# A hybrid GLA, FoX and memory layer on one core: GpSimd in source order in the gates, FoX decay rows loaded and masked in two steps, DRAM sums paced otherwise

## The chip, the cores and the metric

The kernel runs on one core of one Trainium2 chip. The metric is the device time of one execution in microseconds (us). Before the change three runs took 825.73, 826.78 and 827.77 us; their median is 826.78 us. The traces are of single executions, and times within a trace count from its start.

The core's engines run beside each other, each through its own list of instructions, and wait for one another by semaphores. TensorE (PE in the profile) multiplies matrices into PSUM, the memory of its results. VectorE (DVE) and ScalarE (ACT) work element by element on PSUM and SBUF, the main on-chip memory. GpSimd (POOL) does a little of the same and issues DMA transfers, among them those that add what they bring to what stands at the target. SyncE (SP) does nothing but issue transfers.

## The reference, cut to what matters

One layer of an encoder over 512 frames of width 1024: a gated linear attention (GLA), a forgetting attention (FoX) and an attention to 256 memory tokens, merged by three gates, then an output projection and a squared-ReLU MLP. All in float32.

```python
u = rmsnorm(h, g_mix[l])
proj = u @ w_in[l]
(gq, gk, gv, gg, ga, fq, fk, fv, ff, mq, gates) = split_cols(proj, PROJ_SIZES)
...
o_gla = rmsnorm(o_gla, g_gla_head[l]) * jax.nn.silu(gg.reshape(B, S, GLA_HEADS, GLA_DV))
y_gla = o_gla.reshape(B, S, GLA_V) @ w_gla_o[l]
...
# FoX, for each block of 128 queries
s = jnp.einsum('bhqd,bhkd->bhqk', qi, kh).astype(jnp.float32) * scale
s = s + Fi[..., None] - F[:, :, None, :]
mask = k_pos[None, :] <= q_pos[:, None]
p = jax.nn.softmax(jnp.where(mask, s, -jnp.inf), axis=-1)
...
gt = jax.nn.sigmoid(gates.reshape(B, S, N_BRANCH, D))
merged = gt[:, :, 0] * y_gla + gt[:, :, 1] * y_fox + gt[:, :, 2] * y_mem
h = h + merged @ w_out[l]
u2 = rmsnorm(h, g_ffn[l])
h = h + jnp.square(jax.nn.relu(u2 @ w_ff1[l])) @ w_ff2[l]
return rmsnorm(h, g_final)
```

The change touches the FoX scores, the GLA, the three gate projections with their merge, and the beginning of the output projection.

## The kernel before

Precision. Each operand of a matmul is split into a high part (a rounded copy, made by a ScalarE cast: `hi`, `whi`, `f1h`) and a low part (what is left, made by a VectorE subtraction: `lo`, `wlo`, `f1l`). A product is three matmuls, high by high, high by low and low by high (`mm3`, lines 162 to 165). So before TensorE can use a weight tile of 128 by 1024, the tile has to land, be cast (line 153 or 1087) and be subtracted (line 154 or 1091).

Fewer multiplications. The large products are not done block by block but in seven products of sums of blocks, as in Strassen's scheme. So weights are needed in sums: "11", "12", "21" and "22" name the quarters of a weight matrix that such a sum adds up.

Order. TensorE runs in the order of the source. The other engines' lists are put in order by a scheduler, except inside `in_order()` (line 131), which chains each instruction of VectorE, ScalarE and SyncE behind the one before it in the source. All the gates stand inside one such block (line 1237). GpSimd isn't in the chain, and the scheduler orders it.

FoX, about 60 to 150 us of the trace. Eight heads are worked in four pairs j. For head h, `decay_bcast` (line 628) loads a row of decays, broadcast to 128 partitions, into a tile nFb (two buffers) by a DMA that ScalarE issues; the mask is added to it by two VectorE instructions (line 640). `fox_scores(j)` computes the scores of a pair and subtracts nFb, `fox_turn(h)` transposes the probabilities and splits them (PTh, PTl), and `fox_values(h)` multiplies them by V and writes oT (line 703), which is split into ofh and ofl. These steps are listed with a number of filler matmuls each and woven with matmuls of projections. Loads and masks are one step, `fox_rows`.

GLA, about 220 to 295 us, is woven in the same manner from a list of steps with their shares of fillers.

Sums in DRAM. For the MLP some sums of weight blocks are made in DRAM ahead of their use (the tensors T): 40 DMAs of GpSimd, listed by `sum_ops` (line 105), of which 35 come early and five late. `next_sum` (line 115) is called at each weight cast. From the eighth on it lets the next two of the list go, each waiting for that cast. When `late_on` is set, it takes from the five late ones, which also wait for the last merge on GpSimd.

Gates, 296 to 424 us. Three gates g (0 FoX, 1 memory, 2 GLA) take seven rounds n each, in the order 1, 2, 5, 3, 6, 7, 4. A round is two tiles of 128 frames, 24 matmuls. The round (2, 4) is put among the rounds of the GLA output ("Y", 1), ("Y", 0) and of the output projection ("O", 1), ("O", 0). A round reads two weight tiles c. Those of rounds 1, 5, 6, 7 and 4 are built in place in four SBUF tiles wb: `pair[m][c]`, where m is 0 or 1. By their numbers in the listings, wb_473 and wb_474 are pair[0], wb_475 and wb_476 are pair[1]. Gate g builds rounds 1, 5, 6 and 4 in pair[g % 2] and round 7 in the other pair. SyncE loads the first block, and GpSimd adds the others, each by an accumulate DMA (`plus`, line 1073). `low(r, c)`, called a round ahead of the matmuls, makes the low part; behind rounds 1, 5 and 6 it issues the accumulate for the next round on the same tile: "12" behind round 1 (for round 5), "22" behind 5 (for 6), "21" behind 6 (for 4). Behind the matmuls of round 5 the other pair gets its "22", for round 7. The results pass through tiles ct (`evac`) and a tanh. For gates 1 and 2, VectorE multiplies by the branch (line 1167) and GpSimd adds the product to acc (`merge`, line 1168).

Of the kernel before, what the change touches and what calls it, by code (L numbers as in the profile page):

```python
# [58 lines left out]
def hybrid_block(ctx, tc, chunks, wst, memT, xT, xN, gffn, gfin, wup, cst, out):  # L59
    nc = tc.nc  # L60
# [55 lines left out]
    def next_sum(after):  # L116

        chunk_n[0] += 1
        if chunk_n[0] <= 7:
            return  # L120
        for to, src, add_ in islice(sums[len(late_on)], 2):
            with tc.issue_after(merged[0]) if late_on else ExitStack():
                if add_:
                    d = nc.gpsimd.dma_start(to, src, accum_op=ALU.add, max_dma_last_dim=8192)
                else:
                    d = nc.gpsimd.dma_start(to, src)
            tc.add_manual_dep(d.ins, after.name, mybir.DependencyInfo(mybir.DependencyClass.Sync, mybir.DependencyReason.DATA),
                              reason="pace")

    @contextmanager  # L130
    def in_order():

        traced = nc.cur_bb.bb.instructions
        last, behind = traced[-1], {}
        yield
        for i in traced[next(k for k in reversed(range(len(traced))) if traced[k] is last) + 1:]:
            if i.engine in (mybir.EngineType.DVE, mybir.EngineType.Activation, mybir.EngineType.SP):
                if i.engine in behind:
                    tc.add_manual_dep(i, behind[i.engine].name, mybir.DependencyInfo(
                        mybir.DependencyClass.NoSync, mybir.DependencyReason.DATA), reason="order")  # L140
                behind[i.engine] = i
# [360 lines left out]
    with pool("fox") as xp:  # L502
# [122 lines left out]
        live, rows = {}, {}  # L625
# [7 lines left out]
        def fox_rows(j):  # L633
            for e in range(2):
                if j:
                    rows[2 * j + e] = decay_bcast(2 * j + e, nc.scalar)
                nFb = rows[2 * j + e]
                for b in (slice(1, 2), slice(5, 8)):
# [95 lines left out]
        mem_rows()  # L734
        fox_rows(0)
        fox_scores(0)
# [3 lines left out]

        gvg = v_chunks(OFF["gv"], lambda t, ps: nc.scalar.copy(gv[:, t, :], ps))
        T, V_, R, A = fox_turn, fox_values, fox_rows, fox_scores
        steps = [(R, 1, 0), (T, 0, 5), (V_, 0, 0), (T, 1, 5)]
        for j in range(1, 4):
            more = 1 + (j == 3)
            steps += [(A, j, 4 * more), (V_, 2 * j - 1, 5 * more)] + [(R, j + 1, 0)] * (j < 3)
            steps += [(T, 2 * j, 5 * more), (V_, 2 * j, 0), (T, 2 * j + 1, 5 * more)]
        steps.append((V_, 7, 0))
# [129 lines left out]
    with pool("gla") as lp:  # L878
# [115 lines left out]
        def u_lefts():  # L994
# [5 lines left out]
        steps = (  # L1000
            (decays, (0,), 13), (key_turn, (0,), 5), (gla_scores, (0,), 2), (decays, (1,), 9), (key_turn, (1,), 4),
            (gla_values, (0,), 0), (gla_scores, (1,), 8), (gla_turn, (0,), 0), (gla_turn, (1,), 4), (gla_values, (1,), 10),
            (u_lefts, (), 0), (gate_ready, (0,), 0), (gla_turn, (2,), 6), (gate_ready, (1,), 0), (gla_turn, (3,), 0))
# [27 lines left out]
    with pool("outp") as op_:  # L1031
# [204 lines left out]
        hN, now = [], [rounds[0]]  # L1236
        with in_order():
            for n in range(2):
# [4 lines left out]
            for i, r in enumerate(rounds):  # L1243
# [5 lines left out]
                if r == ("Y", 0):  # L1249
                    late_on.append(1)  # L1250
                    hN += [h_tile(t, "h") for t in range(NT)]
# [12 lines left out]
                for t in range(n):  # L1264
# [7 lines left out]
                    if t == 0:  # L1272
                        for x in parts:
                            merge(*x)
                        for x in due:
                            high(*x)
                            low(*x)
                        go(after, i)
                evac(r, n - 1)
        u2j = up.tile([P, 2, 4, 4, 256], F32R, tag="uhl", name="u2")  # L1280
# [747 lines left out]
```

## Time and profile before

| | us |
|---|---|
| median of three runs | 826.78 |
| the profiled execution | 827.7 |
| its span on the core | 825.9 |
| TensorE busy within the span | 800.9 |
| VectorE busy | 607.5 |
| ScalarE busy | 459.6 |
| GpSimd busy | 102.9 |

The profiled execution is 0.9 us above the median. Its span is shorter than its time by 1.8 us, which lie before the first instruction and behind the last. The mean clock granted to TensorE was 0.993 of full speed.

How such rows read. A row of the timeline or of the waits has the start (us), the busy time (us), engine, line, operation, the tile written, an arrow and the tiles read, the shapes, xN for the number of instructions in it, and in brackets the engine's idle time just before it and what ended that. A line such as L1087 is a line of the kernel before; where a helper stands there, several callers share it. An engine with a q (SPq, POOLq) is the queue of a DMA that the engine issued.

### The profile page before, as it was taken

What the parts mean: (1) busy time and instruction counts of PE and PEld (TensorE: products, weight loads), DVE (VectorE), ACT (ScalarE), POOL (GpSimd) and SP (SyncE); (2) the same over time, 40 slices, a digit from 0 to 9 for tenths busy, and PEclk for the clock granted to TensorE, in tenths of its full rate; (3) what the DMA queues carried; (4) which work ended last, traced back from release to release, by engine and by line L of the source; (5) the groups of instructions that cost most, each with busy time, mean ns of one, the idle gap of its engine ahead of it and who ended that gap; (6) DMA issues with size and microseconds to landing.
All of it is one profiled execution on the core that took longest, in us unless ns stands there. A gap on an engine that the chain in (4) does not pass through costs nothing.

```text
span 825.9 us, 11694 instructions
## 1 busy us (share of the span) xinstructions
PE 800.9 (97%) x4375; PEld 681.3 (82%) x4375; DVE 607.5 (74%) x945; ACT 459.6 (56%) x733; POOL 102.9 (12%) x135
## 2 busy tenths in 40 slices
PE   9999999999999998988999999999999999999996
PEld 7788877888888776756888879987998899889985
DVE  6868787375545886567666467879799779888896
ACT  7756655435543445444543347865577466647764
POOL 0001111211100120134301000011001100110011
PEclk9999999999999999999999999999999999999998
DMA  9354879999922229866937932798857865896643
GB/s 357 131 176 178 327 264 240 248 337 246 339 90 77 104 76 203 224 136 196 213 98 257 271 110 102 254 239 204 245 188 170 216 243 167 190 237 229 172 81 124
DMA packets 40489, 164.39 MB, mean 199 GB/s; under 512 B 4848, under 2 KB 5552, under 8 KB 38064
## 3 DMA queue, kind: packets, MB, share of 16 engines
q0 software_dynamic: 10784, 61.87, 34.4%
q1 hardware_dynamic: 28288, 97.81, 32.9%
q10 hardware_dynamic: 1360, 3.96, 1.3%
q8 instruction: 34, 0.56, 0.3%
q14 instruction: 23, 0.19, 0.1%
HBM read 161.50 MB, written 35.68 MB: 239 GB/s over the span
## 4 chain that ended last, share of the span: by engine, by line
PE 45%; DMA 8%; DVE 5%; issue 4%; ACT 2%; POOL 0%; POOLq 0%; SPq 0%; DVEq 0%; ACTq 0%
PE mm L1321 11%; PE mm L164 7%; PE mm L165 7%; PE mm L163 7%; DMA wb<-in_wst_dram 4%; PE a L164 3%; PE a L165 3%; PE a L163 3%; PE mm L1650 3%; DMA b<-in_wst_dram 2%; DMA raw<-in_wst_dram 2%; PE mm L1651 1%; DVE lo L1091 1%; DVE lo L1438 1%; DVE f0l L1091 0%
## 5 line engine op out<-in xcount | busy, mean ns | idle before, releaser
L154 DVE TENSOR_TENSOR wlo<-raw,whi 128x1024 fp32r<-128x1024 f32 x38 | 46.5, 1224 | 39.6 <-ACT whi L153 39.6
L1381 DVE TENSOR_TENSOR lo<-raw,hi 128x1024 fp32r<-128x1024 f32 x52 | 63.5, 1223 | 15.6 <-ACT hi L1380 15.5
L1380 ACT CAST hi<-raw 128x1024 fp32r<-128x1024 f32 x52 | 54.4, 1048 | 35.6 <-PE mm L1321 14.2
L1321 PE MATMUL mm<-u,hi 128*128 128x256 f32 x384 | 65.1, 283 | 0.0
L153 ACT CAST whi<-raw 128x1024 fp32r<-128x1024 f32 x38 | 39.9, 1050 | 43.7 <-PE mm L164 14.7
L1700 POOL DMA_DIRECT2D b<-in_wst_dram x30 | 25.6, 855 | 265.3 <-DVE lo L1381 131.1
L163 PE MATMUL mm<-uhl,whi 128*128 128x512 f32 x144 | 57.6, 400 | 0.0
L1321 PEld LDWEIGHTS mm<-u,hi 128*128 128x128 f32 x384 | 56.8, 191 | 0.3
L165 PE MATMUL mm<-uhl,wlo 128*128 128x512 f32 x144 | 56.3, 391 | 0.0
L164 PE MATMUL mm<-uhl,whi 128*128 128x512 f32 x144 | 56.1, 390 | 0.0
L164 PE MATMUL mm<-lo,ch 128*128 128x512 f32 (+1 forms) x132 | 51.2, 388 | 0.4 <-DVE lo L1381 0.4
L163 PE MATMUL mm<-hi,ch 128*128 128x512 f32 (+1 forms) x132 | 51.0, 386 | 0.0
L165 PE MATMUL mm<-hi,cl 128*128 128x512 f32 (+1 forms) x132 | 50.9, 386 | 0.0
L1321 PE MATMUL mm<-u2s,hi 128*128 128x256 f32 x288 | 47.6, 283 | 0.0
L1321 PE MATMUL mm<-u,lo 128*128 128x256 f32 x192 | 47.5, 283 | 0.0
L1091 DVE TENSOR_TENSOR lo<-wb,hi 128x1024 fp32r<-128x1024 f32 x22 | 30.2, 1384 | 20.8 <-ACT hi L1087 20.7
L1380 ACT CAST hi<-b 128x1024 fp32r<-128x1024 f32 x26 | 27.3, 1048 | 29.3 <-PE mm L165 19.2
L1321 PEld LDWEIGHTS mm<-u2s,hi 128*128 128x128 f32 x288 | 41.8, 192 | 0.3
L1381 DVE TENSOR_TENSOR lo<-b,hi 128x1024 fp32r<-128x1024 f32 x26 | 31.7, 1223 | 10.7 <-ACT hi L1380 10.7
L164 PE MATMUL a<-lo,ch 128*128 128x512 f32 (+1 forms) x96 | 37.2, 388 | 0.8 <-DVE lo L1438 0.8
L163 PE MATMUL a<-hi,ch 128*128 128x512 f32 (+1 forms) x96 | 37.0, 386 | 0.0
L165 PE MATMUL a<-hi,cl 128*128 128x512 f32 (+1 forms) x96 | 37.0, 385 | 0.0
(508 smaller groups left out, 2317.5 us busy)
## 6 DMA issues: line engine op xcount, KB each, us to landing
raw<-in_wst_dram SPq DMA_DIRECT2D x108, 512.0 KB
raw<-T SPq DMA_DIRECT2D x32, 512.0 KB
b<-in_wst_dram POOLq DMA_DIRECT2D x32, 512.0 KB, 5.8
T<-in_wst_dram POOLq DMA_DIRECT2D x12, 1024.0 KB, 17.4
wb<-in_wst_dram POOLq DMA_DIRECT2D x22, 512.0 KB, 6.7
b<-in_wst_dram SPq DMA_DIRECT2D x16, 512.0 KB
T<-in_wst_dram POOLq DMA_DIRECT2D x12, 512.0 KB, 8.8
wb<-in_wst_dram SPq DMA_DIRECT2D x12, 512.0 KB
```

Of the source, the lines that this page charges most:

```text
L153: cast = nc.scalar.copy(hi, raw)
L154: low_now[0] = nc.vector.tensor_tensor(lo, raw, f(hi), op=ALU.subtract).ins
L163: nc.tensor.matmul(ps, lh, rh, start=start, stop=False, skip_group_check=on)
L164: nc.tensor.matmul(ps, lh, rl, start=False, stop=False, skip_group_check=on)
L165: nc.tensor.matmul(ps, ll, rh, start=False, stop=stop, skip_group_check=on)
L1091: nc.vector.tensor_tensor(lo, source(r, c), f(hi), op=ALU.subtract)
L1321: nc.tensor.matmul(ps[:, a, :], x[:, a, k, :], y[:, s, k, :], start=start, stop=stop, skip_group_check=go is not None)
L1380: split_now[0] = nc.scalar.copy(hi, raw).ins
L1381: split_now[1] = nc.vector.tensor_tensor(lo, raw, f(hi), op=ALU.subtract).ins
L1438: return nc.vector.tensor_tensor(lo, raws[n, i], f(hi), op=ALU.subtract).ins
L1650: nc.tensor.matmul(ps, wh[:, a, k, :], u[:, :, k, :], start=k == 0, stop=False, skip_group_check=True)
L1700: nc.gpsimd.dma_start(to[i], wst[index["B", q, i, x]], accum_op=ALU.add)
```

## The change

It has four parts.

- `in_order` takes further engines, and the block of the gates names GpSimd: its accumulates and merges stand in the order of the source there.
- FoX: `fox_rows` only issues the loads of a pair's two decay rows, right behind the scores of the pair before; a new step `fox_masks` adds the masks, behind `fox_values(2j)`.
- GLA: three units of filler, nine matmuls, move from `gla_scores(1)` to `gla_values(0)`.
- DRAM sums: one sum a cast up to the 14th cast and two from the 15th, where it was two from the eighth; the five late ones go one a cast, and from the end of round (2, 7) instead of the start of ("Y", 0).

```diff
--- before.py
+++ after.py
@@ -118,7 +118,7 @@
         chunk_n[0] += 1
         if chunk_n[0] <= 7:
             return
-        for to, src, add_ in islice(sums[len(late_on)], 2):
+        for to, src, add_ in islice(sums[len(late_on)], 1 if late_on or chunk_n[0] <= 14 else 2):
             with tc.issue_after(merged[0]) if late_on else ExitStack():
                 if add_:
                     d = nc.gpsimd.dma_start(to, src, accum_op=ALU.add, max_dma_last_dim=8192)
@@ -128,13 +128,14 @@
                               reason="pace")
 
     @contextmanager
-    def in_order():
-
+    def in_order(*others):
+
+        engines = (mybir.EngineType.DVE, mybir.EngineType.Activation, mybir.EngineType.SP, *others)
         traced = nc.cur_bb.bb.instructions
         last, behind = traced[-1], {}
         yield
         for i in traced[next(k for k in reversed(range(len(traced))) if traced[k] is last) + 1:]:
-            if i.engine in (mybir.EngineType.DVE, mybir.EngineType.Activation, mybir.EngineType.SP):
+            if i.engine in engines:
                 if i.engine in behind:
                     tc.add_manual_dep(i, behind[i.engine].name, mybir.DependencyInfo(
                         mybir.DependencyClass.NoSync, mybir.DependencyReason.DATA), reason="order")
@@ -631,10 +632,12 @@
             return nFb
 
         def fox_rows(j):
-            for e in range(2):
-                if j:
-                    rows[2 * j + e] = decay_bcast(2 * j + e, nc.scalar)
-                nFb = rows[2 * j + e]
+            for h in (2 * j, 2 * j + 1):
+                rows[h] = decay_bcast(h, nc.scalar)
+
+        def fox_masks(j):
+            for h in (2 * j, 2 * j + 1):
+                nFb = rows[h]
                 for b in (slice(1, 2), slice(5, 8)):
                     m = cmask.rearrange("p (o t) -> p o t", o=1).to_broadcast([P, b.stop - b.start, P])
                     nc.vector.tensor_tensor(nFb[:, b, :], nFb[:, b, :], m, op=ALU.add)
@@ -732,19 +735,19 @@
         pair = fox_pair(1)
         next(pair)
         mem_rows()
-        fox_rows(0)
+        fox_masks(0)
         fox_scores(0)
         with tc.issue_after(cast_now[0]):
             mem_split()
         run(pair)
 
         gvg = v_chunks(OFF["gv"], lambda t, ps: nc.scalar.copy(gv[:, t, :], ps))
-        T, V_, R, A = fox_turn, fox_values, fox_rows, fox_scores
-        steps = [(R, 1, 0), (T, 0, 5), (V_, 0, 0), (T, 1, 5)]
+        T, V_, R, A, K = fox_turn, fox_values, fox_rows, fox_scores, fox_masks
+        steps = [(R, 1, 0), (T, 0, 5), (V_, 0, 0), (K, 1, 0), (T, 1, 5)]
         for j in range(1, 4):
             more = 1 + (j == 3)
-            steps += [(A, j, 4 * more), (V_, 2 * j - 1, 5 * more)] + [(R, j + 1, 0)] * (j < 3)
-            steps += [(T, 2 * j, 5 * more), (V_, 2 * j, 0), (T, 2 * j + 1, 5 * more)]
+            steps += [(A, j, 4 * more)] + [(R, j + 1, 0)] * (j < 3) + [(V_, 2 * j - 1, 5 * more)]
+            steps += [(T, 2 * j, 5 * more), (V_, 2 * j, 0)] + [(K, j + 1, 0)] * (j < 3) + [(T, 2 * j + 1, 5 * more)]
         steps.append((V_, 7, 0))
         weave([partial(fn, i) for fn, i, _ in steps], 80, fox_pair(2), gla_k(0), fox_pair(3), gla_q(0), gvg,
               shares=[n for *_, n in steps])
@@ -999,7 +1002,7 @@
 
         steps = (
             (decays, (0,), 13), (key_turn, (0,), 5), (gla_scores, (0,), 2), (decays, (1,), 9), (key_turn, (1,), 4),
-            (gla_values, (0,), 0), (gla_scores, (1,), 8), (gla_turn, (0,), 0), (gla_turn, (1,), 4), (gla_values, (1,), 10),
+            (gla_values, (0,), 3), (gla_scores, (1,), 5), (gla_turn, (0,), 0), (gla_turn, (1,), 4), (gla_values, (1,), 10),
             (u_lefts, (), 0), (gate_ready, (0,), 0), (gla_turn, (2,), 6), (gate_ready, (1,), 0), (gla_turn, (3,), 0))
         weave([partial(fn, *a) for fn, a, _ in steps], 64, gla_k(1), gla_q(1),
               outputs("w_mem_o", omh, oml, ymem), gla_g(2, lp, "og"), gla_g(3, lp, "og"), shares=[n for *_, n in steps])
@@ -1234,7 +1237,7 @@
         split_n[0] = 2
         mh = ml = None
         hN, now = [], [rounds[0]]
-        with in_order():
+        with in_order(mybir.EngineType.Pool):
             for n in range(2):
                 load_sum(0, n, 1)
             for n in range(2):
@@ -1247,7 +1250,6 @@
                     mhp = late.enter_context(pool("mhl"))
                     mh, ml = (mhp.tile([P, KT, S], F32R, name=x) for x in ("mh", "ml"))
                 if r == ("Y", 0):
-                    late_on.append(1)
                     hN += [h_tile(t, "h") for t in range(NT)]
                     gf = hp.tile([P, D], F32, tag="gf", name="gf")
                     for t in (2, 3, 0, 1):
@@ -1276,6 +1278,8 @@
                             high(*x)
                             low(*x)
                         go(after, i)
+                        if r == (2, 7):
+                            late_on.append(1)
                 evac(r, n - 1)
         u2j = up.tile([P, 2, 4, 4, 256], F32R, tag="uhl", name="u2")
         u2 = [u2j[:, i] for i in range(2)]
```

On GpSimd, from the first accumulate of the gates on, the list was this before (wb_473 and wb_474 are pair[0], wb_475 and wb_476 pair[1]):

```order
L1074 DMA wb_475_2995<-in_wst_dram 128x1024
L1074 DMA wb_476_2996<-in_wst_dram 128x1024
L1074 DMA wb_473_2993<-in_wst_dram 128x1024
L1074 DMA wb_474_2994<-in_wst_dram 128x1024
L1074 DMA wb_473_2993<-in_wst_dram 128x1024
L1074 DMA wb_474_2994<-in_wst_dram 128x1024
L1074 DMA wb_473_2993<-in_wst_dram 128x1024
L1074 DMA wb_474_2994<-in_wst_dram 128x1024
L1074 DMA wb_475_2995<-in_wst_dram 128x1024
L1074 DMA wb_476_2996<-in_wst_dram 128x1024
L1074 DMA wb_475_2995<-in_wst_dram 128x1024
L1074 DMA wb_476_2996<-in_wst_dram 128x1024
```

These are, two by two: gate 0's "22" for round 7, its "22" for round 6, its "21"; then gate 1's "22" for round 7, its "12" for round 5, its "22" for round 6. Two merges follow. On the same engine at the same place it is now:

```order
L1077 DMA wb_473_2993<-in_wst_dram 128x1024
L1077 DMA wb_474_2994<-in_wst_dram 128x1024
L1077 DMA wb_475_2995<-in_wst_dram 128x1024
L1077 DMA wb_476_2996<-in_wst_dram 128x1024
L1077 DMA wb_473_2993<-in_wst_dram 128x1024
L1077 DMA wb_474_2994<-in_wst_dram 128x1024
L1077 DMA wb_475_2995<-in_wst_dram 128x1024
L1077 DMA wb_476_2996<-in_wst_dram 128x1024
L1077 DMA wb_475_2995<-in_wst_dram 128x1024
L1077 DMA wb_476_2996<-in_wst_dram 128x1024
L1171 TENSOR_TENSOR acc0_1808<-acc0_1808,ct_526_3324 128x512
L1171 TENSOR_TENSOR acc1_1809<-acc1_1809,ct_526_3324 128x512
```

In gate 0 the two "22" have changed places. In gate 1 the "12" and "22" of pair[1] have moved up by two, the "22" of pair[0] has gone from ahead of them to a place right behind the two merges.

On VectorE, in FoX, between the probabilities of the second pair of heads and the transposes of its second head, the list was this before (nFb: decay rows; oT, ofl: output of the pair before; PTl: low part of the transposed probabilities; wlo: a weight of a projection):

```order
L703 TENSOR_TENSOR oT_132_1010<-a_160_1144,th_161_1153 64x512
L640 TENSOR_TENSOR nFb_166_1180<-nFb_166_1180,cst_s_71 128x128
L640 TENSOR_TENSOR nFb_166_1180<-nFb_166_1180,cst_s_71 128x384
L217 TENSOR_TENSOR ofl0_124<-oT_132_1010,ofh0_120 128x512
L154 TENSOR_TENSOR wlo_205_1390<-raw_203_1387,whi_204_1389 128x1024
L640 TENSOR_TENSOR nFb_167_1184<-nFb_167_1184,cst_s_71 128x128
L640 TENSOR_TENSOR nFb_167_1184<-nFb_167_1184,cst_s_71 128x384
L217 TENSOR_TENSOR PTl_485<-a_168_1188,PTh_484 128x512
```

On the same engine, at the same place, it is now:

```order
L643 TENSOR_TENSOR nFb_160_1143<-nFb_160_1143,cst_s_71 128x128
L643 TENSOR_TENSOR nFb_160_1143<-nFb_160_1143,cst_s_71 128x384
L706 TENSOR_TENSOR oT_132_1006<-a_162_1147,th_163_1156 64x512
L643 TENSOR_TENSOR nFb_161_1145<-nFb_161_1145,cst_s_71 128x128
L643 TENSOR_TENSOR nFb_161_1145<-nFb_161_1145,cst_s_71 128x384
L155 TENSOR_TENSOR wlo_207_1391<-raw_205_1388,whi_206_1390 128x1024
L218 TENSOR_TENSOR ofl0_124<-oT_132_1006,ofh0_120 128x512
L218 TENSOR_TENSOR PTl_485<-a_168_1182,PTh_484 128x512
```

The first mask has moved ahead of oT, and the second ahead of the weight's low part and of ofl. The next pair of heads has the same move.

On ScalarE, at the output projection, where the merged sums are turned and scaled (mh) and the first weights behind them are cast (f0h, f1h, whi), the list was this before:

```order
L1180 ACTIVATE mh_3775<-mm_642_4081 128x4x128
L1180 ACTIVATE mh_3775<-mm_643_4100 128x4x128
L216 CAST f0h_653_4209<-raw_655_4211 128x1024
L1180 ACTIVATE mh_3775<-mm_644_4119 128x4x128
L216 CAST f1h_656_4215<-raw_658_4217 128x1024
L153 CAST whi_660_4223<-raw_659_4221 128x1024
```

On the same engine, at the same place, it is now:

```order
L1183 ACTIVATE mh_3775<-mm_642_4081 128x4x128
L217 CAST f1h_656_4215<-raw_658_4217 128x1024
L1183 ACTIVATE mh_3775<-mm_643_4100 128x4x128
L154 CAST whi_660_4223<-raw_659_4221 128x1024
L217 CAST f0h_653_4209<-raw_655_4211 128x1024
L1183 ACTIVATE mh_3775<-mm_644_4119 128x4x128
```

Two casts that stood behind the last mh now stand ahead of it, one of them ahead of the last but one. TensorE's list differs only in the nine filler matmuls of the GLA, and SyncE's does not differ.

## The prediction

> **What bounds the kernel now.** First the page: its head, the busy shares and the chain that ended last.
>
> ```profile
> span 825.9 us, 11694 instructions
> PE 800.9 (97%) x4375; PEld 681.3 (82%) x4375; DVE 607.5 (74%) x945; ACT 459.6 (56%) x733; POOL 102.9 (12%) x135
> PE 45%; DMA 8%; DVE 5%; issue 4%; ACT 2%; POOL 0%; POOLq 0%; SPq 0%; DVEq 0%; ACTq 0%
> ```
>
> TensorE is busy for 97% of the span and the change leaves all 4375 matmuls, so time can only come from its idle stretches and from stretches at a lower clock. GpSimd is busy for 12%: its order matters only through the transfers that it issues. Next the busy time by stage. The columns are window, length, then busy us and instructions of PE, PEld, DVE, ACT and POOL, then granted clock, DMA share, GB/s.
>
> ```profile
> 296.00:424.00 128.00, 116.24 (x483) 91.86 (x483) 86.07 (x83) 62.89 (x74) 32.06 (x30) 0.97 0.73 173
> 400.00:420.00 20.00, 20.00 (x90) 16.58 (x89) 11.07 (x11) 10.34 (x13) 3.28 (x4) 1.00 0.80 178
> 319.00:324.20 5.20, 2.73 (x9) 1.49 (x9) 2.76 (x3) 3.29 (x4) 0.87 (x2) 1.00 0.63 113
> 351.40:357.40 6.00, 2.62 (x9) 1.35 (x8) 2.62 (x3) 1.81 (x2) 0.86 (x1) 0.98 0.64 150
> 357.20:360.60 3.40, 3.32 (x8) 2.67 (x9) 2.28 (x5) 2.14 (x3) 1.14 (x2) 0.50 0.68 123
> 384.50:387.90 3.40, 3.40 (x10) 2.62 (x9) 2.43 (x4) 2.83 (x3) 1.81 (x3) 0.50 0.92 314
> ```
>
> In the gates (296 to 424) TensorE idles 128.00 − 116.24 = 11.8 us, half of its idle time in the whole span (825.9 − 800.9 = 25.0). The third branch's gates (400 to 420) lose nothing: 90 matmuls in 20.00 us, 0.222 us each, so a round of 24 takes 5.3 us. By that rate the nine matmuls of 319.0 to 324.2 should take 2.0 us and lose 3.2; those of 351.4 to 357.4 lose 4.0; and two stretches of 3.40 us at clock 0.50 lose up to 1.7 us each. So the gates come first. Who is waited for there:
>
> ```profile
> 319.73 0.51 PE L163 MATMUL mm<-hi,f1h 128*128 128x512 f32 x1 [0.69 <-ACT hi L1087]
> 334.88 0.47 PE L163 MATMUL mm<-hi,uhl 128*128 128x512 f32 x1 [1.35 <-DVE ct L1050]
> 352.22 0.50 PE L163 MATMUL mm<-hi,s 128*128 128x512 f32 x1 [0.74 <-ACT hi L1087]
> 365.37 0.50 PE L164 MATMUL mm<-lo,s 128*128 128x512 f32 x1 [0.58 <-DVE lo L1091]
> 383.90 0.47 PE L163 MATMUL mm<-hi,uhl 128*128 128x512 f32 x1 [3.52 <-DVE ct L1050]
> ...
> 318.63 1.05 ACT L1087 CAST hi<-wb 128x1024 fp32r<-128x1024 f32 x1 [4.92 <-DMA wb<-in_wst_dram]
> 321.59 1.05 ACT L1087 CAST hi<-wb 128x1024 fp32r<-128x1024 f32 x1 [1.91 <-DMA wb<-in_wst_dram]
> 351.12 1.05 ACT L1087 CAST hi<-wb 128x1024 fp32r<-128x1024 f32 x1 [4.45 <-DMA wb<-in_wst_dram]
> ```
>
> At 319.7 (round 6 of gate 0) and 352.2 (round 5 of gate 1) the chain is matmul, ScalarE cast, accumulate DMA of GpSimd. At 334.9 and 383.9 (round 4) it is VectorE's evacuation of round 7.
>
> **Part 1, GpSimd in source order in the gates.**
>
> ```profile
> 306.77 0.85 POOL L1074 DMA_DIRECT2D wb<-in_wst_dram  x1 [0.23 <-DVE lo L1091]
> 307.91 0.86 POOL L1074 DMA_DIRECT2D wb<-in_wst_dram  x1 [0.29 <-DVE lo L1091]
> 336.84 0.86 POOL L1074 DMA_DIRECT2D wb<-in_wst_dram  x1 [11.78 <-DMA wb<-in_wst_dram]
> 340.11 2.65 POOL L1074 DMA_DIRECT2D wb<-in_wst_dram  x3 [2.42 <-DMA wb<-in_wst_dram]
> 360.32 3.90 POOL L1168 TENSOR_TENSOR acc<-acc,ct 128x512 f32<-128x512 f32 x2 [1.94 <-DVE ct L1167]
> ...
> DMA to landing us min/median/max: 8.1/10.7/13.6
> DMA to landing us min/median/max: 5.0/5.1/5.1
> ```
>
> The two landing rows are the wb tiles' issues within 304 to 309 and within 353 to 358.5. Gate 0: the four accumulates that begin at 304.70 put pair[1], for round 7, ahead of pair[0], which round 6 waits for at 318.63 and 321.59. Now pair[0] goes first. As two transfers that landed ahead of it now share only what comes behind, I take pair[0] as landing 2 us or more earlier, enough for the 0.69 wait at 319.73 and its three successors. The price is pair[1], which takes pair[0]'s old landings, 318.6 and 321.6; with a cast of 1.05 and a low part (1.22, row below) it is ready at 323.9, and round 7 starts near 328 − 2.8 = 325. The 1.35 at 334.88 stays or grows. Gain 2.0 to 3.8, taken as 2.8.
>
> Gate 1: before, pair[0]'s "22" for round 7 stands first; at 336.84 and 340.11 it waits for the load of its tile, and the "12" for round 5 waits behind it. Now "12" stands first: it is issued about 5 us sooner, so round 5 starts without its wait. The 4.0 lost in 351.4 to 357.4 go, and the half clock that followed, up to 1.7. The clock is full until these waits and falls at their end. What is late next is low parts that stand beside GpSimd's merges, and round 4's wait:
>
> ```profile
> 337.67 1.22 DVE L1091 TENSOR_TENSOR lo<-wb,hi 128x1024 fp32r<-128x1024 f32 x1
> 360.76 4.56 DVE L1091 TENSOR_TENSOR lo<-raw,hi 128x1024 fp32r<-128x1024 f32 x2
> 374.98 0.59 ACT L1147 COPY ct<-mm 128x512 f32<-128x512 f32 x1 [2.13 <-PE mm L165]
> ```
>
> The low part takes 4.56 / 2 = 2.28 us beside the merge of 360.32 and 1.22 alone, so the 0.58 at 365.37 stays. From round 6's copy at 374.98 to round 4's start at 383.90 VectorE works through a chain of 8.9 us in the same order as before: the 3.52 and the second half clock stay. Gate 1 gains 5.9 (bounds 1.6, the last two waits having grown, to 6.1). Gate 2 has no wait to lose. **Gates: 2.8 + 5.9 = 8.7, bounds 3.6 to 9.9.**
>
> A rule of the Trainium skill speaks against the 1.7 in this: "TensorE: Matmul & The Clock Gate", section "Part 1: The HAM clock gate (the "warmup" mystery)", puts half rate after at least one idle window of about 3.4 us. By that rule the dip at 357.2 would have another cause, as TensorE was busy for 2.62 of the 6.00 us ahead of it, and the gates would give 7.0; the trace, where the dip stands right behind those waits, differs from the rule.
>
> **Part 2, the FoX masks.**
>
> ```profile
> 103.65 0.76 DVE L640 TENSOR_TENSOR nFb<-nFb,cst_s 128x128 f32<-128x128 f32 x2 [2.93 <-DMA nFb<-dF]
> 106.85 1.29 DVE L217 TENSOR_TENSOR PTl<-a,PTh 128x512 fp32r<-128x512 f32 x2
> 107.59 0.50 PE L695 MATMUL a<-PTl,V 128*128 128x512 f32 x1 [1.32 <-DVE PTl L217]
> 124.93 0.76 DVE L640 TENSOR_TENSOR nFb<-nFb,cst_s 128x128 f32<-128x128 f32 x2 [1.30 <-DMA nFb<-dF]
> 127.75 0.50 PE L695 MATMUL a<-PTl,V 128*128 128x512 f32 x1 [0.20 <-DVE PTl L217]
> 100.02 0.69 DVE L703 TENSOR_TENSOR oT<-a,th 64x512 f32<-64x512 f32 x1
> ```
>
> The masks wait for their row's DMA and hold what TensorE needs. Now they stand ahead of oT. If the rows land as before, the order from 103.65 is masks 0.76, oT 0.69, masks 0.76, a weight low part 1.22, ofl 0.69, in all 4.1: PTl begins at 107.8 instead of 106.85, and in the next pair at 129.0 instead of about 127.0: −0.9 and −2.0. If they land by 100.0 both gaps go: +1.5. The DRAM sums issued by then are halved, so I take +0.6, near the better end, since the first landing needs 3.6 us.
>
> **Part 3, GLA fillers.** Nine matmuls (2.0 us) move from before a PSUM wait to another place.
>
> ```profile
> 271.83 0.50 PE L163 MATMUL mm<-whi,om 128*128 128x512 f32 x1 [0.92 <-DVE at L947]
> 481.81 0.50 PE L164 MATMUL mm<-wlo,mh 128*128 128x512 f32 x1 [0.76 <-DVE wlo L154]
> 445.19 3.32 POOL L124 DMA_DIRECT2D T<-in_wst_dram  x4 [32.25 <-ACT hi L1087]
> 469.91 1.05 ACT L216 CAST f1h<-raw 128x1024 fp32r<-128x1024 f32 x1 [3.04 <-DMA raw<-in_wst_dram]
> 474.23 1.05 ACT L153 CAST whi<-raw 128x1024 fp32r<-128x1024 f32 x1 [3.27 <-DMA raw<-in_wst_dram]
> 440.17 36.72 SPq L146 DMA_DIRECT2D raw<-in_wst_dram  x8
> 238.42 0.12 POOL L897 MEMSET ex<- 128x8 f32 x1 [17.17 <-ACT ex L895]
> ```
>
> The 0.92 at 271.83 is a wait for the masked copy (line 947) to free a PSUM buffer. The waiting matmul now has nine fillers more ahead of it, which would cover all of it; but VectorE has the next head group's small operations ahead of that copy, so I take half: +0.4 (from −0.3, when those operations cost more than the fillers cover, to +0.9).
>
> **Part 4, the sums.** SyncE issues this part's eight weight loads from 440.17 on, and four sums of 445.19 run beside them. With one sum for each cast from round (2, 4) on, the five go at about 426 to 444, mostly ahead of the loads; the casts at 469.91 and 474.23, which wait 3.04 and 3.27 us for their loads, come sooner, and the 0.76 at 481.81 goes: +0.7. But those casts, of f1h and whi, now stand ahead of evacuations of the turned sums (mh) on ScalarE. Where the loads land no sooner, TensorE waits for mh behind a wait of 3 us, of which the idle time before them covers about one: −2.0 to +1.0. The early sums end with the 28th weight cast, which by the casts' times stands near 234, instead of the 25th near 205. Behind them on GpSimd stands a fill at 238.42 that VectorE needs for the keys; two accumulates of 0.5 us and two fills of 0.5 end by 236, so I put 0, and about one us for each us by which the last sum waits beyond that for the sum under it.
>
> **Sum.** 8.7 + 0.6 + 0.4 + 0.7 = 10.4. The profiled execution took 827.7 (span 825.9 and 1.8 around it), giving 817.3; the runs' median, 826.8, is 0.9 lower: **816.5**.
>
> **The rivals.** *Casts and masks stall*: DMA lands no sooner, FoX gives −2.9 and the late part −2.0, leaving 8.7 + 0.4 − 4.9 = 4.2: 822.6. For it: 2.93 and 3.04 us of waits for DMA at just these instructions. The Trainium skill's "DMA: Bandwidth & Descriptors", section "Queues, rings and completion order", says a DMA engine takes turns between queues packet by packet; by that rule a row gets the same share however many sums stand in GpSimd's queue, and this is the rival it gives. *Slow accumulates*: the "12" lands after 10.7 us as at 304 to 309, not 5.1, so about 5 of gate 1 is lost: 821.5. *The order is not the limit*, or does nothing: VectorE's chain takes the place of each wait, leaving the 1.7 of parts 2 to 4: 825.1. *Slower, GpSimd's head of line*: pair[0]'s "22" of gate 1 now stands behind the two merges that end at 364.2; moved by 2.8 + 5.0 that is 356.4. Round 7, at 374.9 − 8.7 = 366.2, needs it cast, so it must land by 365, 8.7 us later. Against it: 5.1 in the nearest row. At 13.6 it costs 5 us; it makes the kernel slower from 19 us on, and at 24, by 15.3 − 10.4 = 4.9, 831.7.
>
> **How the numbers follow.** Forecast 0.68; stalls 0.12; slow accumulates 0.11; order not the limit 0.04; slower 0.05. All terms at their best give 9.9 + 1.5 + 0.9 + 1.0 = 13.3, 813.5; runs scatter by 1. The range goes from 812.5 to 823.5 with both middle rivals. A difference of 0.3%, 2.5 us, is about what a measurement here can tell: faster 0.88, same 0.07 (with 0.03 for both middle rivals at once), slower 0.05.
>
> **What would show it.** Right: no waits of TensorE for hi or lo in rounds 6 of gate 0 and 5 of gate 1, clock 1.00 there, one dip left before round 4 of gate 1, and the GpSimd accumulate for round 5 issued before 340. Wrong: a wait of round 7 for hi, masks whose wait stays near 3 us, a TensorE wait for mh near 470, or a gap moved one round on.

## The result and the profile after

The changed kernel took 818.48 us, the median of four runs (816.45 to 818.88), beside 826.25 us of the kernel before. The ratio is 0.9898, with a 95% interval from 0.9876 to 0.992: 1% faster. A second measurement of the same kernel, among the experiments, gave 0.9911 (0.9884 to 0.9938). Forecast were 816.5 us in a range from 812.5 to 823.5. The gain is 7.8 us where 10.4 were forecast.

The page of the changed kernel begins so, and the windows below it have the columns of those shown before (PE, PEld, DVE, ACT, POOL, then clock, DMA share, GB/s):

```profile
span 817.1 us, 11695 instructions
PE 798.7 (98%) x4375; PEld 681.3 (83%) x4375; DVE 606.6 (74%) x945; ACT 459.3 (56%) x733; POOL 104.9 (13%) x135
...
296.00:415.00 119.00, 112.02 (x475) 90.02 (x474) 82.80 (x82) 61.86 (x74) 34.33 (x30) 0.97 0.77 186
315.00:320.00 5.00, 5.00 (x24) 4.12 (x23) 4.97 (x5) 2.47 (x3) 1.21 (x2) 1.00 1.06 261
346.00:352.00 6.00, 6.00 (x29) 4.95 (x28) 3.96 (x7) 2.51 (x3) 2.36 (x3) 1.00 0.80 158
375.60:381.60 6.00, 5.93 (x14) 4.70 (x15) 4.88 (x5) 3.29 (x4) 3.58 (x2) 0.51 0.49 175
```

The gates' idle time fell from 11.8 to 7.0 us (119.00 − 112.02). In round 6 of gate 0 (315 to 320) and in round 5 of gate 1 (346 to 352) TensorE now works without a pause, and the half clock of 357 to 360 is gone. The half clock at the start of round 4 of gate 1 (from 375 us now) is still there, and in this profile it has become longer. Four of the waits that TensorE still has, two rows of ScalarE that belong to the first of them, and part of GpSimd's list beside them:

```profile
324.81 0.50 PE L164 MATMUL mm<-hi,uhl 128*128 128x512 f32 x1 [0.39 <-ACT ct L1150]
323.22 1.05 ACT L1090 CAST f0h<-wb 128x1024 fp32r<-128x1024 f32 x1 [1.42 <-DMA wb<-in_wst_dram]
324.18 1.07 ACT L1150 COPY ct<-mm 128x512 f32<-128x512 f32 x2
...
332.17 0.47 PE L164 MATMUL mm<-hi,uhl 128*128 128x512 f32 x1 [1.63 <-DVE ct L1053]
356.42 0.50 PE L165 MATMUL mm<-lo,s 128*128 128x512 f32 x1 [0.58 <-DVE lo L1094]
375.67 0.77 PE L164 MATMUL mm<-hi,uhl 128*128 128x512 f32 x1 [3.79 <-DVE ct L1053]
...
336.47 0.86 POOL L1077 DMA_DIRECT2D wb<-in_wst_dram  x1 [15.95 <-DVE lo L1094]
351.37 3.91 POOL L1171 TENSOR_TENSOR acc<-acc,ct 128x512 f32<-128x512 f32 x2 [2.95 <-DVE ct L1170]
355.23 1.76 POOL L1077 DMA_DIRECT2D wb<-in_wst_dram  x2
```

The "12" of gate 1 is issued at 336.47, as soon as its tile's low part is made. The "22" of pair[0] follows the merges at 355.23 and 355.8; by the trace these two land 5.5 and 8.6 us later, in time for round 7 but for 0.4 us, as told further down.

TensorE runs the same list in both kernels but for the nine fillers, so the two traces can be laid beside each other matmul by matmul. The start of a matmul in a trace minus the start of the same one in the trace of before is called its shift here. The gain of a stage is by how much the shift falls across it. Each number is a median over some ten or more us; "again" is the second profile of the changed kernel.

| stage (us in the trace before) | forecast | changed kernel | again |
|---|---|---|---|
| ahead of FoX (to 95) | 0 | −0.3 | 0.0 |
| FoX (95 to 135) | +0.6 | +0.1 | −1.8 |
| GLA and early sums (135 to 290) | +0.4 | +0.3 | −1.6 |
| gate 0 (290 to 330) | +2.8 | +2.9 | +3.2 |
| gate 1 (330 to 393) | +5.9 | +4.1 | +5.8 |
| output projection (393 to 490) | +0.7 | +1.1 | +1.1 |
| behind it (490 on) | 0 | +0.6 | +1.3 |
| sum | +10.4 | +8.8 | +8.0 |

The wait of 0.39 at 324.81 is new. In round 7 of gate 0 TensorE waits for the copy of round 6's result (ct), which stands on ScalarE behind the cast of pair[1]; and the second tile of pair[1], now last of the four on GpSimd, landed only at 323.1. In the changed kernel's first profile gate 0 gains 3.6 us up to that point and loses 0.7 there.

### The profile page after: what moved, and what is told of

The parts are those of the page before. It is cut to its first block, busy times and chain, and to the rows that moved or that the text cites. A ratio compares the mean times of both kernels' runs of the same rounds, so it can differ in the third digit from the quotient of the medians.

```text
span 817.1 us, 11695 instructions
## 1 busy us (share of the span) xinstructions
PE 798.7 (98%) x4375; PEld 681.3 (83%) x4375; DVE 606.6 (74%) x945; ACT 459.3 (56%) x733; POOL 104.9 (13%) x135
## 4 chain that ended last, share of the span: by engine, by line
PE 75%; DMA 9%; DVE 6%; issue 5%; ACT 3%; POOL 1%; POOLq 0%; DVEq 0%; ACTq 0%
PE mm L1325 14%; PE mm L164 12%; PE mm L165 12%; PE mm L166 12%; PE a L164 4%; PE a L166 4%; PE a L165 4%; DMA wb<-in_wst_dram 4%; PE mm L1654 3%; DMA raw<-in_wst_dram 3%; PE mm L385 1%; DMA b<-in_wst_dram 1%; PE mm L1655 1%; PE a L398 1%; DVE wlo L155 1%
## 5 line engine op out<-in xcount | busy, mean ns | idle before, releaser
L154 ACT CAST whi<-raw 128x1024 fp32r<-128x1024 f32 x38 | 39.9, 1050 | 44.2 <-PE mm L165 14.3
```

The lines of the kernel that those rows point to most:

```text
L154: cast = nc.scalar.copy(hi, raw)
```

## The experiments

Eleven kernels were run, each beside the kernel before on the same chip. The kernel before spread more there than at first (824 to 832 us), so the ratios have wide intervals, and differences between variants are read from shifts.

### One part alone, and the change without that part

`a1_order_only` is the kernel before with GpSimd in source order in the gates and nothing else.

```diff
-    def in_order():
+    def in_order(*others):
...
-        with in_order():
+        with in_order(mybir.EngineType.Pool):
```

> The kernel before with one part of the change alone: GpSimd in source order in the gates. If that order carries the gain, it saves what TensorE's shift in the gates shows in the changed kernel, 2.9 us in gate 0 and 4.1 in gate 1: about 7.0 us less than before, near 819.2. If the accumulates land in time only because the sums are spaced otherwise, it saves 4 us or less, and waits for hi return in round 5 of gate 1. TensorE's shift before 290 us is 0 by either.

818.33 us, ratio 0.9882 (0.9855 to 0.9909): the whole gain of the change. The shift falls by 3.6 us in gate 0 and by 6.2 in gate 1; no wait for hi is left in these rounds. FoX and the sums are as in the kernel before here, so the accumulates land in time without the new spacing.

`a2_no_order` is the changed kernel without it.

```diff
-        with in_order(mybir.EngineType.Pool):
+        with in_order():
```

> The changed kernel without GpSimd's source order: FoX, GLA and sums as changed. If the order carries the gain, about 1.6 us less than before remain, 824.6, all of it behind 470 us, and the waits of 319 to 324 and 351 to 357 us are back. If the sums' spacing carries it, 4 us or more remain, with the accumulates of gate 1's round 5 landing earlier than in the kernel before.

827.53 us, ratio 0.9985 (0.9968 to 1.0002): 1.6 us below the 829.09 of the kernel before, as expected, but the interval takes in no difference. The waits are back, as its timeline of TensorE shows:

```profile
321.73 0.50 PE L164 MATMUL mm<-hi,f1h 128*128 128x512 f32 x1 [1.78 <-ACT hi L1090]
356.10 0.50 PE L164 MATMUL mm<-f0h,s 128*128 128x512 f32 x1 [1.06 <-ACT f0h L1090]
357.36 0.50 PE L165 MATMUL mm<-f0l,s 128*128 128x512 f32 x1 [0.76 <-DVE f0l L1094]
```

The two runs together show that the order of GpSimd's accumulates carries the gain and that the other three parts bring nothing that these runs can tell.

### The sums in DRAM

`a3_early_sums_back` paces the early sums as before.

```diff
-        for to, src, add_ in islice(sums[len(late_on)], 1 if late_on or chunk_n[0] <= 14 else 2):
+        for to, src, add_ in islice(sums[len(late_on)], 1 if late_on else 2):
```

> The changed kernel with the early sums two a cast from the eighth cast on, as before. If each sum waits 5 to 6 us on GpSimd for the sum under it and so holds the fill that the keys need (242.86 against 238.42 us), the fill is back at 238 and TensorE gains 0.4 to 0.8 us by 255 us; FoX's decay rows land 0.9 and 1.8 us later than in the changed kernel and its two waits are those of before, 0.3 us worse to no worse. Sum: 0 to 0.8 us faster than the changed kernel. If the fill has slack, no difference behind 255 us, and 0.3 slower in FoX.

819.21 us, ratio 0.9876 (0.9845 to 0.9908). From the time, no difference from the changed kernel can be told. By shifts GLA (200 to 290 us) gains 0.8 us, half a microsecond more than in the changed kernel; over the table's whole stage, from 135 us on, it is 0.3 in both, as this run loses 0.5 near 193 us. FoX loses 2.6, much more than the 0.3 expected: the first pair's rows take 7.7 us from issue to mask (6.7 before), TensorE waits 2.34 us for PTl at 109.19, and a half clock follows. First the GLA. These are rows of the changed kernel, on GpSimd and then on VectorE:

```profile
229.29 0.49 POOL L126 DMA_DIRECT2D T<-T  x1 [5.45 <-DMA T<-in_wst_dram]
235.74 0.49 POOL L126 DMA_DIRECT2D T<-T  x1 [5.96 <-DMA T<-in_wst_dram]
241.46 0.49 POOL L126 DMA_DIRECT2D T<-T  x1 [5.23 <-DMA T<-in_wst_dram]
242.86 0.14 POOL L900 MEMSET ex<- 128x8 f32 x1
...
243.03 0.69 DVE L903 TENSOR_TENSOR kn<-gkT,ex 128x512 f32<-128x512 f32 x1 [5.11 <-POOL ex L900]
```

Each of the last sums waits on GpSimd for the sum under it to land, 5 to 6 us, so the list ends 7 us behind its last cast. The fill of ex stands behind it, 4.4 us later than before (238.42), and VectorE waits 5.11 us for it. In `a3_early_sums_back` the last sum is issued at 219.4, and the fill waits for its own operand, not for sums. TensorE's wait that follows is 0.23 us in the changed kernel's profile, 2.04 in its second one, and 3.15 in `b1_fox_back`, which has the same spacing; by shift TensorE loses 0.5, 2.3 and 5.0 us there, the last with a half clock behind the wait:

```profile
253.71 0.49 PE L889 MATMUL a<-cst_s,la 128*128 128x128 f32 x2 [0.23 <-DVE at L950]
...
257.13 0.60 PE L889 MATMUL a<-cst_s,la 128*128 128x128 f32 x3 [2.04 <-DVE at L950]
...
257.62 0.60 PE L887 MATMUL a<-cst_s,la 128*128 128x128 f32 x3 [3.15 <-DVE at L948]
```

`b1_fox_back` is the changed kernel with FoX's loads and masks in one step again.

```diff
-            for h in (2 * j, 2 * j + 1):
-                rows[h] = decay_bcast(h, nc.scalar)
-
-        def fox_masks(j):
             for h in (2 * j, 2 * j + 1):
+                if j:
+                    rows[h] = decay_bcast(h, nc.scalar)
                 nFb = rows[h]
...
-            steps += [(A, j, 4 * more)] + [(R, j + 1, 0)] * (j < 3) + [(V_, 2 * j - 1, 5 * more)]
-            steps += [(T, 2 * j, 5 * more), (V_, 2 * j, 0)] + [(K, j + 1, 0)] * (j < 3) + [(T, 2 * j + 1, 5 * more)]
+            steps += [(A, j, 4 * more), (V_, 2 * j - 1, 5 * more)] + [(R, j + 1, 0)] * (j < 3)
+            steps += [(T, 2 * j, 5 * more), (V_, 2 * j, 0), (T, 2 * j + 1, 5 * more)]
```

> The changed kernel with FoX's loads and masks in one step again, the new spacing of the sums kept. If the spacing decides when the decay rows land, TensorE's shift between 100 and 130 us stays within 0.5 us of the changed kernel's and the time is the same. If the split brought the rows 0.9 and 1.8 us sooner, it goes: both waits for PTl grow by about these, 1 to 2.5 us slower.

817.87 us, ratio 0.9878 (0.9844 to 0.9912). In FoX it loses 0.6 us by shift, the changed kernel gains 0.1 or loses 1.8: no effect of the split can be told. What follows are the first loads of the second pair of rows shown in the prediction, and the masks that wait for them, in the kernel before (load alone), the changed kernel and `b1_fox_back`:

```profile
117.12 0.33 ACTq L630 DMA_DIRECT2D nFb<-dF  x1
...
117.09 0.33 ACTq L631 DMA_DIRECT2D nFb<-dF  x1
123.14 0.76 DVE L643 TENSOR_TENSOR nFb<-nFb,cst_s 128x128 f32<-128x128 f32 x2 [2.86 <-DMA nFb<-dF]
127.18 1.29 DVE L218 TENSOR_TENSOR PTl<-a,PTh 128x512 fp32r<-128x512 f32 x2
...
117.97 0.33 ACTq L631 DMA_DIRECT2D nFb<-dF  x1
124.14 0.76 DVE L641 TENSOR_TENSOR nFb<-nFb,cst_s 128x128 f32<-128x128 f32 x2 [2.99 <-DMA nFb<-dF]
```

From issue to mask it takes 124.93 − 117.12 = 7.8 us before, 6.1 with the split and the new spacing, 6.2 with the new spacing alone, and 7.8 with the split and the old spacing (`a3_early_sums_back`). So the spacing brings the rows sooner. But PTl begins at 127.18, as it did before (127.00): what the rows gain, the masks take by standing ahead of oT. That place, too, comes with the spacing: in `a3_early_sums_back`, which has the split and the old spacing, the scheduler puts the masks behind oT.

`a4_late_sums_back` paces the five late sums as before.

```diff
-        for to, src, add_ in islice(sums[len(late_on)], 1 if late_on or chunk_n[0] <= 14 else 2):
+        for to, src, add_ in islice(sums[len(late_on)], 1 if not late_on and chunk_n[0] <= 14 else 2):
...
                 if r == ("Y", 0):
+                    late_on.append(1)
...
-                        if r == (2, 7):
-                            late_on.append(1)
```

> The changed kernel with the five late sums as before: two a cast, from the start of round (Y, 0). If the 1.1 us that TensorE gains near 483 us come from these sums leaving the DMA engines, they go: 1.1 us slower than the changed kernel, with the wait of 0.76 us for wlo back. If they come from the other order of ScalarE's casts, that order tells: wherever the casts of f1h and whi stand ahead of the last mh, the gain stays.

819.75 us, ratio 0.9896 (0.9866 to 0.9926). The shift falls by 0.2 us up to 490 us instead of 1.1, and the wait is back:

```profile
473.03 0.50 PE L165 MATMUL mm<-wlo,mh 128*128 128x512 f32 x1 [0.64 <-DVE wlo L155]
```

So the gain there comes with the sums' times. It isn't shown that they bring it alone: ScalarE's order went back with them, with the casts of f1h and whi (461.14 and 465.45) behind the last mh (457.71) again, where in the changed kernel (460.41 and 462.47) they stand ahead of it (464.38). No run has the one without the other. Behind 490 us this run gains 2.1 where the changed kernel gains 0.6 and 1.3, so the total doesn't tell.

### The fillers of the GLA

`b2_gla_back` puts them back.

```diff
-            (gla_values, (0,), 3), (gla_scores, (1,), 5), (gla_turn, (0,), 0), (gla_turn, (1,), 4), (gla_values, (1,), 10),
+            (gla_values, (0,), 0), (gla_scores, (1,), 8), (gla_turn, (0,), 0), (gla_turn, (1,), 4), (gla_values, (1,), 10),
```

> The changed kernel with the nine GLA fillers at their old place. If they cover the wait for a PSUM buffer near 272 us, it is back with 0.9 us, and the late fill of 242.9 us shows as well: 0.8 to 1.6 us slower than the changed kernel by 275 us. If they only move the wait, no difference.

818.96 us, ratio 0.9879 (0.9858 to 0.9899). The shift rises by 1.25 us in this stage, where it falls by 0.28 in the changed kernel, and both waits show:

```profile
255.11 0.60 PE L889 MATMUL a<-cst_s,la 128*128 128x128 f32 x3 [0.99 <-DVE at L950]
273.92 0.50 PE L164 MATMUL mm<-whi,om 128*128 128x512 f32 x1 [0.92 <-DVE at L950]
```

The fillers cover the second wait in full, 0.92 us; by shift the changed kernel gains 0.8 there. The 0.99 is the late fill.

### The wait that is left in the gates

VectorE's list ahead of round 4 of gate 1 in the changed kernel:

```profile
369.20 1.30 DVE L1170 SCALAR_TENSOR_TENSOR ct<-ct,ymem 128x512 f32<-128x512 f32 x2 [1.13 <-ACT ct L1125]
370.41 2.31 DVE L1094 TENSOR_TENSOR lo<-wb,hi 128x1024 fp32r<-128x1024 f32 x1
372.65 2.28 DVE L1094 TENSOR_TENSOR f0l<-wb,f0h 128x1024 fp32r<-128x1024 f32 x1
374.85 1.27 DVE L1053 TENSOR_TENSOR ct<-ct,mm 128x512 f32<-128x512 f32 x2
```

The evacuations that TensorE waits for stand last, behind two products and two low parts. GpSimd adds the products beside these low parts, which take 2.3 us instead of 1.22. The Trainium skill's "GPSIMD Engine Reference", section "1. Specifications", says that GpSimd shares its SBUF interfaces with VectorE and contends there with VectorE instructions that have two SBUF inputs; the trace agrees, 2.31 against 1.22.

`b6_round7` writes the rounds 7 otherwise: evacuate the first tile, then the low parts, then evacuate the second tile, then merge. `d1_order_round7` is the kernel before with the order of `a1_order_only` and these lines.

```diff
                     mms(r, t)
-                    if t:
+                    if t and not (n == 2 and r[1] == 7):
                         evac(r, t - 1)
+                    if t == 0 and r[1] == 7:
+                        evac(r, 0)
...
-                        for x in parts:
-                            merge(*x)
+                        if r[1] != 7:
+                            for x in parts:
+                                merge(*x)
...
                 evac(r, n - 1)
+                if r[1] == 7:
+                    for x in parts:
+                        merge(*x)
```

> The changed kernel with VectorE's list in the rounds 7 written otherwise: evacuation of the first tile as soon as TensorE ends it, then the two low parts, the evacuation of the second tile, and the merges with GpSimd's adds last. If the wait of 3.79 us ahead of round 4 of gate 1 is VectorE's chain (two products, two low parts slowed by the merges, two evacuations), the low parts take 1.22 instead of 2.3 us, the evacuations end by 374.2 instead of 376.1, TensorE's waits ahead of the rounds 4 of gates 0 and 1 (1.63 and 3.79) fall below 0.6 each, and the half clock goes: 4 to 7 us faster than the changed kernel. If the weights' landing decides (cast at 371.1), 2 us or less.

> The kernel before with GpSimd in source order and the same new list of VectorE in the rounds 7, with FoX, GLA and sums as before. If the other parts of the change bring nothing together, it is as fast as the changed kernel with that list, within 2 us. If they bring the 1 to 2 us of the sums and the fillers, it is slower by these.

816.68 us, ratio 0.9856 (0.9831 to 0.9881), and 817.91, ratio 0.9859 (0.9839 to 0.9879). The waits ahead of both rounds 4 are gone, and the low parts take 1.23. But of 5.2 us by which the shift fell there in `b6_round7`, 5.4 came back in the next round, where the low parts now stand behind four products:

```profile
369.11 1.23 DVE L1094 TENSOR_TENSOR lo<-wb,hi 128x1024 fp32r<-128x1024 f32 x1
371.36 1.23 DVE L1094 TENSOR_TENSOR f0l<-wb,f0h 128x1024 fp32r<-128x1024 f32 x1 [1.02 <-ACT f0h L1090]
373.10 4.68 DVE L1170 SCALAR_TENSOR_TENSOR ct<-ct,ymem 128x512 f32<-128x512 f32 x4
377.70 4.52 DVE L1094 TENSOR_TENSOR lo<-wb,hi 128x1024 fp32r<-128x1024 f32 x2
...
380.04 0.50 PE L165 MATMUL mm<-lo,uhl 128*128 128x512 f32 x1 [3.02 <-DVE lo L1094]
```

The mechanism was right, but of the 4 to 7 us expected of `b6_round7` against the changed kernel the profiles show 3.2 or 4.0 (its shift at the end is −12.0, against −8.8 and −8.0 in the changed kernel's two): the wait moved on. `d1_order_round7` is within 2 us of `b6_round7`, as it would be if the other parts bring nothing.

`e1_merges_end` is the changed kernel with the evacuations of `b6_round7` and the merges at the end of every round. `e2_all` also holds the masks behind the second oT of their step and paces the early sums by the line of `a3_early_sums_back`. These are the lines on the merges, then those on the masks.

```diff
                     if t == 0:
-                        for x in parts:
-                            merge(*x)
                         for x in due:
...
                 evac(r, n - 1)
+                for x in parts:
+                    merge(*x)
```

```diff
-            nc.vector.tensor_tensor(oT[a], po[a], th[a], op=ALU.add)
+            live["last"] = nc.vector.tensor_tensor(oT[a], po[a], th[a], op=ALU.add).ins
...
+                    with tc.issue_after(live["last"]) if "last" in live else ExitStack():
                         nc.vector.tensor_tensor(nFb[:, b, :], nFb[:, b, :], m, op=ALU.add)
```

> The changed kernel with the list of VectorE in rounds 7 as in the run before, and the merges at the end of every round, behind the next round's low parts. If the 3.0 and 0.4 us ahead of round 1 of gate 2 are those low parts standing behind four products of merges, they fall below 1 us in all, the wait of 0.6 in round 3 of gate 1 goes, and the gates end 2 to 4 us earlier than with rounds 7 alone: 4 to 7 us faster than the changed kernel. If VectorE and GpSimd have too much to do in rounds 7, 4 and 1 in whatever order, the wait moves on by a round and the time is that of rounds 7 alone.

> As the run with all merges at the end, with the masks held behind the second oT of their step and the early sums two a cast as before the change. If the two waits of FoX come from masks that stand ahead of PTl, both go, 1.5 us by 130 us, though the rows land later again; if the fill of the keys is on time, near 239 to 242 us, no wait for it follows by 258 us: 1.5 to 2.5 us faster than with the merges alone. If a mask behind the second oT is late for the scores, a wait shows near 115 or 135 us instead.

813.41 us, ratio 0.9849 (0.9818 to 0.988), and **809.80 us, ratio 0.9795 (0.9771 to 0.9819)**: the second beats both kernels. The first is 6.6 us below the 820.00 of the changed kernel beside it, within the 4 to 7 expected; the second is another 3.6 faster, more than the 1.5 to 2.5 expected. By shifts the gates, up to 424 us, gain 14.1 and 14.3 us in the two, where they gain 7.0 and 8.9 in the changed kernel's profiles. Of the second, the gates, one row of the masks and the fill:

```profile
290.00:408.00 118.00, 115.81 (x503) 93.18 (x503) 88.03 (x91) 63.37 (x76) 35.07 (x31) 1.00 0.78 188
...
109.43 1.41 DVE L644 TENSOR_TENSOR nFb<-nFb,cst_s 128x128 f32<-128x128 f32 x4
...
238.48 0.12 POOL L901 MEMSET ex<- 128x8 f32 x1 [17.16 <-ACT ex L899]
```

TensorE idles 2.2 us in the gates (118.00 − 115.81), and its clock is 1.00 throughout. The masks no longer wait for their rows, neither wait for PTl is left, and the fill is in time. By shifts FoX gains 1.4 us and GLA (200 to 290 us) 0.8; 0.6 are lost between them, near 193 us.

`e3_after_again` is the changed kernel once more.

> The changed kernel itself, for a comparison on this chip and for what varies between executions: the half-clock stretch ahead of round 4 of gate 1 (between 5 and 13 matmuls long in the runs so far) and the wait for the late fill near 255 us (0.2 to 1.0). Within 1.5 us of its first time relative to the kernel before.

820.00 us, ratio 0.9911 (0.9884 to 0.9938). Its profile is the column "again" of the table.

## Why the prediction was right, point by point

- **The gates, 8.7.** Right in mechanism and place: 7.0 in the first profile, 8.9 in the second, and 9.8 with the order alone, where gate 2 gives 0.8 back. Its two terms for gate 1, 4.0 and 1.7, add up to 5.7, not to the 5.9 taken. Pair[0] of gate 0 came sooner, and the wait of round 4 grew from 1.35 to 1.63 us, inside "stays or grows". That gate 0 gave 2.9 for the 2.8 taken is in part luck: it gained 3.6, and the price, pair[1], which had been put at nothing with a landing at 321.6, cost 0.7 with one at 323.1. Gate 1's first half gained the 5.9 forecast in each of the three (the shift falls from −2.99 to −8.90 in the first). What was mis-sized is the wait of round 4 that "stays" with its half clock: in the first profile the wait grew from 3.52 to 3.79, and the first 30 matmuls behind it took 9.6 us instead of 8.5, as 13 instead of 8 of them ran at half clock. That is 1.4 of the 1.8 us missing there. The other 0.4 are lost at the start of round 7 (366.15): its first matmul waits for a copy on ScalarE that stands behind the cast of pair[0]'s second tile (364.56). In the second profile those 30 matmuls took 8.5 again, and the term came out at 5.8.
- **The half clock of 357 to 360.** It is gone, with the waits ahead of it, in all eleven profiles that have the order. That these waits caused it isn't shown: it stands in the one profile of the kernel before, but in `a2_no_order` TensorE waits 1.78, 0.76 and 0.77 us between 319 and 326 and 1.06 and 0.76 near 357, and its clock stays at 1.00. So between the prediction's reading and the rule of the Trainium skill's "TensorE: Matmul & The Clock Gate", section "Part 1: The HAM clock gate (the "warmup" mystery)", an idle window of about 3.4 us, these runs don't decide for this dip. The 7.0 that the prediction gave the gates by that rule was measured in the first profile, but by chance: the dip did go, and other losses, named above, took its place.
- **FoX, +0.6: failed.** The step that failed is the reading that rows that land sooner empty the gaps. They do land 1.1 and 1.8 us sooner, but not by 100, and the masks' new place ahead of oT uses that up. Of the two ends, −2.9 and +1.5, the value lies between; the second profile is 1.8 below zero mostly because a half clock followed one of these waits (1.3).
- **The early sums, 0: failed.** The prediction took the list's end from the last cast, 234, and named a later end only as a risk, "each us by which the last sum waits beyond that for the sum under it". Each of them does wait, 5 to 6 us. The fill came 4.4 us late, which costs TensorE 0.5 us in the first profile, 2.3 in the second and 5.0 in `b1_fox_back`. The waits of T for T stood in the trace before (last sum at 215.11 behind the cast of 204.7) and weren't carried over.
- **The fillers, +0.4.** They cover 0.92, twice the value taken; the late fill took much of it back. That the stage came out at 0.3 in the first profile, near the 0.4 forecast, is luck; in the second it lost 1.6.
- **The late sums, +0.7.** 1.1 measured, and the old spacing brings the wait back, together with the old order of casts.
- **The rivals.** Slow accumulates: no, the two tiles of "12" land 5.1 and 6.8 us after their issues. Stalls: half, the masks still wait 2.5 and 2.9 us, but no TensorE wait for mh appears. The head of GpSimd's line: pair[0]'s second tile lands at 364.5, half a microsecond before the 365 from which it was to cost, and yet round 7 starts 0.4 late behind its cast; in the second profile it costs nothing. That cast could begin only when its target was free as well, and by the trace the two came within 0.02 us, so which one held it is not told. The order not being the limit: refuted by the first two experiments.

## What to carry to other kernels

Where one engine issues transfers for several consumers, the order of its list is a schedule of DMA: a transfer that waits for its buffer holds back all that stand behind it, so list them by when they are needed and look at each wait of the issuing engine. When a wait goes, look at what the same engine does in the next two rounds: moving merges out of one round sent the wait on until every round had its work in the order low parts, evacuations, merges. A slower pace doesn't end at its last trigger when its steps wait for one another; carry their waits from the trace into the estimate.

## What was not expected of the hardware

The nine waits of 3.50 to 3.79 us ahead of round 4 of gate 1, in nine profiles, all had a half clock behind or within them. For the shorter waits here, it isn't tied to their length. The changed kernel's two profiles have nearly the same wait near 107.6 us (1.02 and 1.13), but TensorE's clock behind it was full in one and half in the other (the third number from the end of each row of windows; the first row is of the changed kernel, the second of its repeat):

```profile
109.00:111.00 2.00, 2.00 (x17) 1.82 (x15) 1.80 (x4) 1.76 (x4) 0.00 (x0) 1.00 0.02 8
...
109.00:111.00 2.00, 2.00 (x11) 2.00 (x11) 1.41 (x3) 0.89 (x2) 0.00 (x0) 0.50 0.06 23
```

In `d1_order_round7` a wait of 3.04 us had no half clock behind it; in `b6_round7` one of 3.02 at the same place had. The kernel before had none behind 1.32 us. The Trainium skill's "TensorE: Matmul & The Clock Gate", section "Part 1: The HAM clock gate (the "warmup" mystery)", asks for an idle window of about 3.4 us and calls the window free-running. The nine long waits agree with the first, and the half clock after 1.13 us differs from it; that the window runs freely would fit the same program doing both, but no run here varied its phase alone. In `e2_all`, where no wait is longer than 0.5 us once TensorE has started, none appears from 7 us up to its last matmul.
